# A hybrid attention layer on one core: the gate's activation ahead of the next x split in the first sweep, and a small transpose moved back in the output stage

## The chip, the core and the metric

The kernel runs on one core of one Trainium2 chip. The metric is the time of one execution in device microseconds (us), and the median of several runs is compared. The engines are called as in the profile: PE is TensorE, PEld its weight loads, ACT is ScalarE, DVE is VectorE, POOL is GpSimd, and SP is the engine that issues most of the DMAs.

## What is computed

One encoder layer over x with 2048 rows of 1024 numbers, all in float32. `x @ w_in` is cut by columns into the inputs of two groups of heads. Group A is gated linear attention in both directions over chunks of 64 positions, with a decay for each key dimension that comes from a product of low rank (`lr`), and a SiLU gate. Group B is latent attention with softmax over all positions, and a SiLU gate. Cut to what matters here:

```python
h = x @ w_in
g_q, g_k, g_v, g_gate, g_lr_f, g_lr_b, m_cq, m_ckv, m_kr, m_gate = split(h)
# group A, per direction
log_a = log_sigmoid(lr @ wg2 + bg) / 16
b = cumsum(log_a)                      # inside a chunk
q_dec, k_dec, k_tail = q * exp(b), k * exp(-b), k * exp(b_last - b)
o = mask(q_dec @ k_dec.T) @ v + q_dec @ state
state = state * exp(b_last) + k_tail.T @ v
o_a = rms_norm(o_fwd + o_bwd) * silu(gate)
# group B
o_b = softmax(q_nope @ k_nope.T + q_rope @ k_rope.T) @ v * silu(m_gate)
out = layer_norm(alpha * x + concat(o_a, o_b) @ w_out)
```

## The kernel before

**Number format.** [...]

**Stages.** The first sweep (`sweep_a`, to about 352 us) goes over the 16 tiles of 128 rows of x from the last to the first: step `i` works on tile `c = 15 - i`. It makes the inputs of group A and runs its forward half. A second sweep (to about 632 us) makes the inputs of group B and runs the backward half. Attention follows, 16 blocks of one head by 512 queries, block after block, and last the product with `w_out` and the LayerNorm, whose first parts run between the last block's work.

**A step of the first sweep.** For its tile it runs three product groups on PE, each over eight slices `k` of 128 of the 1024 input columns: `ipa_0` (288 columns: the decay's input `lr`, then `q`), `ipa_1` (384 columns: `k` and a part of `v`) and `ipa_2` (384 columns of `v`). Except for the tiles 15, 14 and 0, a fourth product `ipg` (512 columns: the gate) follows. Behind the three groups' products come copies out of PSUM: `ga_lr` copies `lr` in three pieces, `ga_q2` copies `q`. The four products take their PSUM banks in turn from one pool of two buffers, so the tile of `ipa_1` lies in the bank that `ipg` of the step before had. `gate_end` runs `silu` on `ipg`: three ACT passes (lines 1491, 1493, 1495) and a multiplication on DVE (line 1497) that reads `ipg` once more; the tile of the result is `gs`.

**Work between the products.** The smaller work of group A is called between the products at places that the table `STEPS_A` names: a key `(g, k)` means behind slice `k` of product group `g`, and each entry is a part and whether it belongs to the current step or to the one before it. `ga_q` transposes the copy of `q` on PE (`qT`), multiplies by the decay on DVE (`qd`, line 943), stores `qd` in four DMAs, and splits it into `qbh` and `qbl`, each in two halves. `ga_k` does the same for `kd` (line 967), `kh` and `kl`. `ga_kt` transposes `kd` (`kt`) and splits it. `ga_lrT` transposes `lr` and copies it out (`lrTs`), and `ga_z` multiplies it by the decay's weights (`z`). `ga_intra` is the masked product `Ap` of queries and keys, `ga_state` the product `Up` of keys and values. In the steps 5 to 9 of this loop parts of the rotary embedding's angles run too, and behind step 9 the sine and cosine tables, with two ACT table loads.

**The x tile.** At the head of step `i` the loop loads tile `i + 1` of x (`ga_ld`, into `xaf`) and splits it (`ga_x`): `xah` on ACT, `xal` on POOL. The last step does the same for the first tile of the second sweep (`xlate`).

**What sets the order.** The steps 0 to 3 follow a list written out by hand (`ORDER_A`). From step 4 on, each engine's order comes from the framework's scheduler at compile time, which starts from the order in the program and may move an instruction ahead of others; `self.after(i)` forbids it to put what is issued inside ahead of instruction `i`.

**The output stage.** In attention the order is written out by the table `PLACE`: for each part of a block a place in units of pairs of score products, behind the block's end for the late parts; a program sorts all parts by their places. Block 14 is the last but one. Its row sums are transposed in two small matmuls (`sx`, `tsum`, line 1658), reduced on DVE (line 1667) and inverted (`rc`, line 1669). `turn` (line 1680) transposes the four columns of reciprocals to four rows (`rt`); `rows` copies them on ACT (line 1686) and stores them on SP (line 1687). `y` is the block's product with the values' weights, and `yc` copies and stores it. `sx`, `y` and `rt` of that block take one PSUM bank in turn. `wof` (line 1848) is the load of the next slice of `w_out`, and `po` are the first parts of the output product.

## Time and profile before

| | |
|---|---|
| timed runs | 1296.20, 1297.36, 1297.93 us; median 1297.36 us |
| profiled execution | 1299.13 us, of which the span of the trace is 1296.9 us |
| busy, share of the span | PE 98%, PEld 86%, DVE 70%, ACT 65%, POOL 61% |
| granted clock of PE, mean over the span | 0.998 |
| instructions on PE | 6988 matmuls, 6988 weight loads |
| mean DMA rate over the span | 112 GB/s |

The windows of the profile give the stages. Each row is a stretch, its length, and the busy time of PE, PEld, DVE, ACT and POOL with their instructions, then the granted clock, the DMA share and GB/s:

```profile
22.00:132.00 110.00, 108.54 (x693) 103.22 (x693) 74.13 (x146) 71.86 (x159) 35.28 (x24) 1.00 0.30 92
132.00:352.00 220.00, 219.05 (x1358) 204.76 (x1358) 120.44 (x249) 131.72 (x284) 72.98 (x59) 1.00 0.27 81
1105.00:1297.00 192.00, 183.74 (x828) 152.68 (x828) 118.60 (x184) 54.10 (x141) 98.45 (x63) 0.98 0.55 176
```

The first two are the first sweep from its second step on, the last is the output stage. In a row of a timeline the first number is the start in us from the start of the span, the second the duration, and what stands in brackets is the idle time ahead of the instruction on its engine and what ended it. A matmul's duration reaches to its modelled end, so the next one starts before it is over; what a matmul costs PE is the distance between two starts.

### The profile page before, as it was taken

How to read it: one execution, taken by the hardware profiler on the slowest of the kernel's cores; microseconds unless marked ns; L12 is line 12 of the kernel's file. 1: busy time of each engine (PE TensorE's matmuls, PEld its weight loads, DVE VectorE, ACT ScalarE, POOL GpSimd, SP SyncE). 2: the span in 40 equal slices, each digit the busy share in tenths (PEclk: the TensorE clock that was granted, in tenths of full speed). 3: DMA queues.
4: the chain of work that ended last, by engine and by line, in shares of the span. 5: the costliest groups of instructions: out<-in, count | busy, mean ns of one | idle time of the engine just before them, and what ended most of it. 6: DMA issues, size and time to landing. Idle time of an engine off the chain costs nothing.

```text
span 1296.9 us, 19995 instructions
## 1 busy us (share of the span) xinstructions
PE 1270.2 (98%) x6988; PEld 1119.6 (86%) x6988; DVE 908.5 (70%) x1678; ACT 842.7 (65%) x1482; POOL 790.9 (61%) x500
## 2 busy tenths in 40 slices
PE   7999999999999999999999999999999999999997
PEld 7999999999889999999788888888888888788886
DVE  6865564445675455555898888888888888468655
ACT  7765657555675656655688888888888887523221
POOL 0243232232567666671288888889999999846550
PEclk9999999999999999999999999999999999999999
DMA  8232213131565555565401111122233110367752
GB/s 287 70 94 59 88 55 93 51 96 50 179 224 170 193 200 179 189 213 168 138 1 41 42 41 41 41 63 60 58 90 90 42 41 9 122 197 238 238 170 75
DMA packets 113444, 145.81 MB, mean 112 GB/s; under 512 B 17494, under 2 KB 70110, under 8 KB 113344
## 3 DMA queue, kind: packets, MB, share of 16 engines
q1 hardware_dynamic: 105184, 142.42, 34.9%
q0 software_dynamic: 768, 2.10, 0.4%
q8 instruction: 55, 0.90, 0.3%
q10 hardware_dynamic: 7392, 0.03, 0.3%
q14 instruction: 45, 0.37, 0.1%
HBM read 94.14 MB, written 50.36 MB: 111 GB/s over the span
## 4 chain that ended last, share of the span: by engine, by line
PE 86%; ACT 3%; DVE 2%; POOL 2%; issue 2%; DMA 1%; SPq 0%; DVEq 0%; ACTq 0%; POOLq 0%
PE o L424 4%; PE o L426 4%; PE pS L1535 4%; PE o L425 4%; PE pS L1537 4%; PE pS L1536 4%; PE pS L1538 4%; PE pS L1539 4%; PE ipa L424 4%; PE ipa L426 3%; PE ipa L425 3%; PE po L426 2%; PE po L425 2%; PE po L424 2%; PE pz L425 2%; PE pz L426 2%
## 5 line engine op out<-in xcount | busy, mean ns | idle before, releaser
L376 POOL TENSOR_TENSOR pl<-s,ph 128x1024 fp32r<-128x1024 f32 x128 | 306.3, 2417 | 58.0 <-ACT ph L370 58.0
L1557 DVE TENSOR_TENSOR rm<-pS,rm 128x512 f32<-128x512 f32 x210 | 144.8, 690 | 26.3 <-ACT s L1544 20.7
L1581 DVE TENSOR_TENSOR s<-s,mb 128x1024 f32<-128x1024 f32 x128 | 151.2, 1213 | 9.4 <-PE mb L1575 9.3
L1544 ACT ACTIVATE s<-pS 128x1024 f32<-128x1024 f32 x128 | 131.3, 1026 | 38.0 <-PE pS L1539 33.4
L1044 POOL TENSOR_TENSOR Us<-Us,cw 128x512 f32<-128x512 f32 x16 | 18.6, 1164 | 213.1 <-DVE Us L1042 181.3
L370 ACT ACTIVATE ph<-s 128x1024 fp32r<-128x1024 f32 x128 | 135.2, 1058 | 17.6 <-PE o L426 16.9
L1585 ACT ACTIVATE s<-s 128x1024 f32<-128x1024 f32 x128 | 131.5, 1051 | 13.4 <-DVE s L1581 13.3
L424 PE MATMUL ipa<-wah,xah 128*128 128x384 f32 (+1 forms) x384 | 131.1, 341 | 7.3 <-ACT wah L370 6.8
L425 PE MATMUL ipa<-wal,xah 128*128 128x384 f32 (+1 forms) x384 | 125.8, 327 | 0.2 <-DVE wal L376 0.2
L426 PE MATMUL ipa<-wah,xal 128*128 128x384 f32 (+1 forms) x384 | 125.0, 325 | 0.0
L1535 PE MATMUL pS<-qh,ckvT_h 128*128 128x512 f32 x256 | 102.5, 401 | 0.8 <-DVE rm L1557 0.4
L424 PE MATMUL o<-ph,vh 128*128 128x512 f32 x256 | 101.0, 395 | 0.0
L1536 PE MATMUL pS<-ql,ckvT_h 128*128 128x512 f32 x256 | 99.8, 390 | 0.0
L1538 PE MATMUL pS<-rh,krs 128*128 128x512 f32 x256 | 99.8, 390 | 0.0
L1537 PE MATMUL pS<-qh,ckvT_l 128*128 128x512 f32 x256 | 99.8, 390 | 0.0
L426 PE MATMUL o<-ph,vl 128*128 128x512 f32 x256 | 99.8, 390 | 0.0
L1539 PE MATMUL pS<-rl,krs 128*128 128x512 f32 x256 | 99.8, 390 | 0.0
L425 PE MATMUL o<-pl,vh 128*128 128x512 f32 x256 | 99.7, 390 | 0.0
L1608 DVE TENSOR_TENSOR ap<-ap,s 128x512 f32<-128x512 f32 x120 | 83.1, 692 | 7.1 <-ACT s L1585 4.5
L424 PEld LDWEIGHTS ipa<-wah,xah 128*128 128x128 f32 x384 | 73.1, 190 | 10.4 <-ACT wah L370 7.0
L376 POOL TENSOR_TENSOR ol<-of,oh 128x512 fp32r<-128x512 f32 x32 | 43.6, 1363 | 54.2 <-ACT oh L370 54.2
L424 PE MATMUL pz<-xch,wzh 128*128 128x256 f32 x256 | 74.8, 292 | 0.0
(327 smaller groups left out, 3830.1 us busy)
## 6 DMA issues: line engine op xcount, KB each, us to landing
xcf<-xT_dram SPq DMA_DIRECT2D x16, 512.0 KB, 5.3
xr<-x_dram SPq DMA_DIRECT2D x16, 512.0 KB, 5.7
out_dram<-rr SPq DMA_DIRECT2D x32, 256.0 KB, 4.9
xaf<-xT_dram SPq DMA_DIRECT2D x14, 512.0 KB, 3.8
oib<-oi_s SPq DMA_DIRECT2D x16, 256.0 KB, 3.8
qdb<-qd_s SPq DMA_DIRECT2D x16, 256.0 KB, 4.9
SU<-su_s SPq DMA_DIRECT2D x16, 256.0 KB, 4.1
ub<-u_s SPq DMA_DIRECT2D x16, 256.0 KB, 4.1
```

What stands on the lines that cost most here:

```text
L370: return nc.scalar.activation(dst, src, AF.Copy).ins
L376: return e.tensor_tensor(dst, src, hi.bitcast(F32), ALU.subtract).ins
L424: mm(out, ah, bh, start=start, stop=False)
L425: mm(out, ah, bl, start=False, stop=False)
L426: mm(out, al, bh, start=False, stop=stop)
L1535: mm(ps[:, e], kh, qh, start=True, stop=False)
L1536: mm(ps[:, e], kh, ql, start=False, stop=False)
L1537: mm(ps[:, e], kl, qh, start=False, stop=False)
L1538: mm(ps[:, e], kr, rh, start=False, stop=False)
L1539: mm(ps[:, e], kr, rl, start=False, stop=True)
L1557: V.tensor_tensor(d["rm"], src[:, e], d["rm"], ALU.max)
L1581: V.tensor_tensor(s, s, d["mb"][:, None, :].to_broadcast([P, 2, QB]), ALU.subtract)
```

## The change

It has three parts. First, in the loop steps of the first sweep only the load of the next x tile stays at the head of the step. Its split moves into a new part `next_x` behind slice 1 of `ipa_0`, and may not be put ahead of the last of the gate's three ACT passes. The multiplication `qd` may not be put ahead of the gate's multiplication on DVE. Second, `ga_q` and `ga_k` are cut in two. The transposes, the multiplications and the stores (`q1`, `k1`) stay behind slice 4 of `ipa_0`; the splits (`q3`, `k3`) go behind slice 1 of `ipa_1`, and `qbh` and `qbl` may not be put ahead of the copies of `lr`. Third, two places in `PLACE` put `turn` and `rows` of block 14 later.

```diff
-STEPS_A = {(0, 4): [("q", "prev"), ("k", "prev")], (1, 3): [("kt", "prev"), ("lrT", "cur")],
+STEPS_A = {(0, 1): [("next_x", "cur")], (0, 4): [("q1", "prev"), ("k1", "prev")], (1, 1): [("q3", "prev"), ("k3", "prev")], (1, 3): [("kt", "prev"), ("lrT", "cur")],
...
-    turn=13.6,
-    rows=13.65,
+    turn=17.5,
+    rows=17.55,
...
-                c = ch[i]["c"]
-                if c > 0:
-                    for f in (self.ga_ld, self.ga_x):
-                        for _ in f(i + 1):
-                            pass
+                if ch[i]["c"] > 0:
+                    for _ in self.ga_ld(i + 1):
+                        pass
                 else:
-                    self.xlate = [self.split_x(xp, self.load_x(NCH - 1, "xb"), NCH - 1, "xb")]
+                    self.xlate = self.load_x(NCH - 1, "xb")
...
-            self.hi(lr[:, 64:96], pt[:, 0:32])
+            h = self.hi(lr[:, 64:96], pt[:, 0:32])
             yield
-            self.lo(lr[:, 32:64], pt[:, 0:32], lr[:, 0:32])
+            self.lr_last = h, self.lo(lr[:, 32:64], pt[:, 0:32], lr[:, 0:32])
...
+    def ga_next_x(self, d):
+
+        with self.after(self.gate_act):
+            if d["c"] > 0:
+                for _ in self.ga_x(d["i"] + 1):
+                    pass
+            else:
+                self.xlate = [self.split_x(self.xab, self.xlate, NCH - 1, "xb")]
         yield
...
+        with self.after(*([self.gate_dve] if d["i"] > 3 else [])):
+            nc.vector.scalar_tensor_tensor(two(qd), qT[:, None, 0:2].to_broadcast([P, 2, 2, P]), 0.125, two(d["E1"]),
+                                           ALU.mult, ALU.mult)
...
+    def ga_q3(self, d):
+        qd, qbh, qbl = d["qd"], d["qbh"], d["qbl"]
         halves = (slice(0, 64), 0), (slice(64, 128), 1)
+        lr = self.lr_last if 3 < d["i"] < NCH - 1 else ()
         for r, j in halves:
-            self.hi(qbh[r, :, j], qd[r])
+            with self.after(*lr[:1]):
+                self.hi(qbh[r, :, j], qd[r])
             yield
         for r, j in halves:
-            self.lo(qbl[r, :, j], qd[r], qbh[r, :, j])
+            with self.after(*lr[1:]):
+                self.lo(qbl[r, :, j], qd[r], qbh[r, :, j])
             yield
...
-        self.nc.scalar.activation(t, t, AF.Exp, scale=-1.0)
+        self.gate_act = nc.scalar.activation(t, t, AF.Exp, scale=-1.0).ins
         yield 2
-        nc.vector.tensor_tensor(t, g, t, ALU.mult)
+        self.gate_dve = nc.vector.tensor_tensor(t, g, t, ALU.mult).ins
```

In the pieces below, what an instruction writes stands ahead of the arrow, the number at the end of a name counts the tile, and `x2` means that two like it follow each other. Line numbers behind the change are higher by up to 25. The first pair is ACT in an ordinary step of the first sweep, between the end of one gate product and the middle of `ipa_1`. Before:

```order
L370 ACTIVATE xah_2885<-xaf_2883 128x1024
L1491 ACTIVATE gs_2877<-ipg_2839 128x512
L1493 ACTIVATE gs_2877<-gs_2877 128x512
L1495 ACTIVATE gs_2877<-gs_2877 128x512
L370 ACTIVATE qbh_222<-qd_2908 64x4x128 x2
L370 ACTIVATE lr_221<-ipa_0_2889 128x32 x2
L370 ACTIVATE kh_2923<-kd_2921 128x512
L370 ACTIVATE q_4_2939<-ipa_0_2889 128x256
L370 ACTIVATE kth_2959<-kt_2954 128x2x4x64
```

and now, at the same place:

```order
L1516 ACTIVATE gs_2877<-ipg_2839 128x512
L1518 ACTIVATE gs_2877<-gs_2877 128x512
L1520 ACTIVATE gs_2877<-gs_2877 128x512
L370 ACTIVATE xah_2892<-xaf_2883 128x1024
L370 ACTIVATE lr_221<-ipa_0_2885 128x32 x2
L370 ACTIVATE qbh_222<-qd_2908 64x4x128
L370 ACTIVATE q_4_2931<-ipa_0_2885 128x256
L370 ACTIVATE qbh_222<-qd_2908 64x4x128
L370 ACTIVATE kh_2944<-kd_2917 128x512
L370 ACTIVATE kth_2959<-kt_2954 128x2x4x64
```

The split's copy `xah` has gone behind the gate's three passes, and the two copies of `lr` and the copy of `q` ahead of one half of `qbh` or both. DVE at the same place, before:

```order
L943 SCALAR_TENSOR_TENSOR qd_2908<-qT_2905,E_5_2745 128x512
L1497 TENSOR_TENSOR gs_2877<-ipg_2839,gs_2877 128x512
L967 TENSOR_TENSOR kd_2921<-kT_2918,E_5_2755 128x512
L376 TENSOR_TENSOR qbl_223<-qd_2908,qbh_222 64x4x128 x2
L376 TENSOR_TENSOR kl_2925<-kd_2921,kh_2923 128x512
L376 TENSOR_TENSOR lr_221<-ipa_0_2889,lr_221 128x32
```

and now:

```order
L1522 TENSOR_TENSOR gs_2877<-ipg_2839,gs_2877 128x512
L955 SCALAR_TENSOR_TENSOR qd_2908<-qT_2905,E_5_2745 128x512
L989 TENSOR_TENSOR kd_2917<-kT_2914,E_5_2755 128x512
L376 TENSOR_TENSOR lr_221<-ipa_0_2885,lr_221 128x32
L376 TENSOR_TENSOR qbl_223<-qd_2908,qbh_222 64x4x128 x2
L376 TENSOR_TENSOR kl_2946<-kd_2917,kh_2944 128x512
```

The gate's multiplication has changed places with `qd`, and the small subtraction of `lr` has gone from behind the three splits to ahead of them. The last pair is PE around `rt` of block 14, in the last block of attention. Before:

```order
L1658 MATMUL sx_12231<-ident,acc_12090 128x128 x2
L1680 MATMUL rt_12242<-ident,rc_12238 4x128
L424 MATMUL po_12135<-woh_10769,oh_0_11238 128x512
L425 MATMUL po_12135<-wol_10848,oh_0_11238 128x512
L426 MATMUL po_12135<-woh_10769,ol_0_11297 128x512
```

and now:

```order
L424 MATMUL o_12291<-ph_0_12214,vh 128x512
L425 MATMUL o_12291<-pl_0_12267,vh 128x512
L426 MATMUL o_12291<-ph_0_12214,vl 128x512
L1705 MATMUL rt_12298<-ident,rc_12238 4x128
L424 MATMUL o_12291<-ph_1_12242,vh 128x512
L425 MATMUL o_12291<-pl_1_12306,vh 128x512
```

`rt` has gone from right behind `sx` to behind `y` and a dozen further `po`, between two value products `o` of the last block. On SP the store of `rt` stood ahead of the load `wof`, and the store of `yc` came behind both; now the order is `wof`, `yc`, `rt`.

More of the change, by code (lines that the diff above doesn't have):

```diff
@@ L810, in ga_x @@
         self.lo(xl[:, :, 0], xf, xh[:, :, 0], "dve" if i < 4 else "pool")
+        yield
+    def ga_next_x(self, d):
[5 more added lines that the diff above has]
+                self.xlate = [self.split_x(self.xab, self.xlate, NCH - 1, "xb")]
         yield
@@ L933, in ga_q, with ga_q1 @@
     def ga_q(self, d):
+        yield from self.ga_q1(d)
+        yield from self.ga_q3(d)
+    def ga_q1(self, d):
         nc, c = self.nc, d["c"]
-        qbh, qbl = d["qbh"], d["qbl"]
         qT = d["tr"].tile([P, H, P], F32, tag="tr", name=f"qT{c}")
@@ L940, in ga_q @@
         yield
-        qd = self.t512(d, "qd")
+        qd = d["qd"] = self.t512(d, "qd")
         two = lambda t: t.rearrange("p (r q) t -> p r q t", r=2)
-        nc.vector.scalar_tensor_tensor(two(qd), qT[:, None, 0:2].to_broadcast([P, 2, 2, P]), 0.125, two(d["E1"]),
-                                       ALU.mult, ALU.mult)
+        with self.after(*([self.gate_dve] if d["i"] > 3 else [])):
+            nc.vector.scalar_tensor_tensor(two(qd), qT[:, None, 0:2].to_broadcast([P, 2, 2, P]), 0.125, two(d["E1"]),
+                                           ALU.mult, ALU.mult)
         dst = self.qd_s[c].rearrange("(r d) (q g t) -> r g d q t", r=2, q=2, g=2)
@@ L949, in ga_q, with ga_k1 @@
         yield
+    def ga_q3(self, d):
+        qd, qbh, qbl = d["qd"], d["qbh"], d["qbl"]
         halves = (slice(0, 64), 0), (slice(64, 128), 1)
+        lr = self.lr_last if 3 < d["i"] < NCH - 1 else ()
         for r, j in halves:
-            self.hi(qbh[r, :, j], qd[r])
+            with self.after(*lr[:1]):
+                self.hi(qbh[r, :, j], qd[r])
             yield
         for r, j in halves:
-            self.lo(qbl[r, :, j], qd[r], qbh[r, :, j])
+            with self.after(*lr[1:]):
+                self.lo(qbl[r, :, j], qd[r], qbh[r, :, j])
             yield
     def ga_k(self, d):
+        yield from self.ga_k1(d)
+        yield from self.ga_k3(d)
+    def ga_k1(self, d):
         nc, c = self.nc, d["c"]
@@ L968, in ga_k, with ga_k3 @@
         yield
+    def ga_k3(self, d):
+        kd = d["kd"]
         kh = d["kh"] = self.t512(d, "kh", dt=F32R)
@@ L1494, in silu @@
         yield 1
-        nc.scalar.activation(t, t, AF.Exp, scale=-1.0)
+        self.gate_act = nc.scalar.activation(t, t, AF.Exp, scale=-1.0).ins
         yield 2
-        nc.vector.tensor_tensor(t, g, t, ALU.mult)
+        self.gate_dve = nc.vector.tensor_tensor(t, g, t, ALU.mult).ins
         yield 3
```

## The prediction

> **What bounds the kernel now.** I read the page's busy times first, then the waits of TensorE, then the timelines of one sweep step and of the stretch around the moved transpose, last the windows with the granted clock.

> ```profile
> PE 1270.2 (98%) x6988; PEld 1119.6 (86%) x6988; DVE 908.5 (70%) x1678; ACT 842.7 (65%) x1482; POOL 790.9 (61%) x500
> ```

> TensorE (PE) is busy 98% of the span: 26.7 us are all that it stands. So an edit gains what it takes from PE's standing time, and loses what it adds there. The waits (who waited for whom: total us, times, longest) of PE's weight loads and of its matmuls name two that the change touches.

> ```profile
> PEld ipa L424 <- DVE gs L1497: 2.8, 12, 0.7
> PE rt L1680 <- DVE rc L1669: 3.3, 1, 3.3
> ```

> The first comes once in each of 12 sweep steps: `ipa_1` takes the PSUM bank that the gate product `ipg` of the step before filled, and DVE's `gs` multiplication is that bank's last reader. One such step (start, duration):

> ```profile
> 239.37 0.39 PE L426 MATMUL ipg<-wgh,xal 128*128 128x512 f32 x1
> 239.57 1.06 ACT L370 ACTIVATE xah<-xaf 128x1024 fp32r<-128x1024 f32 x1 [1.97 <-PE ipg L425]
> 240.53 0.58 ACT L1491 ACTIVATE gs<-ipg 128x512 f32<-128x512 f32 x1
> 240.76 2.40 POOL L376 TENSOR_TENSOR xal<-xaf,xah 128x1024 fp32r<-128x1024 f32 x1 [2.05 <-ACT xah L370]
> 241.81 0.63 ACT L1495 ACTIVATE gs<-gs 128x512 f32<-128x512 f32 x1
> 242.60 0.68 DVE L1497 TENSOR_TENSOR gs<-ipg,gs 128x512 f32<-128x512 f32 x1
> 243.09 0.30 PE L426 MATMUL ipa<-wah,xal 128*128 128x288 f32 x1
> 243.34 0.44 PE L424 MATMUL ipa<-wah,xah 128*128 128x384 f32 x1
> 243.62 0.34 PE L425 MATMUL ipa<-wal,xah 128*128 128x384 f32 x1
> 243.79 0.34 PE L426 MATMUL ipa<-wah,xal 128*128 128x384 f32 x1
> ```

> The split's first pass `xah` stands ahead of the gate's three passes, and DVE's `gs` ends at 243.28. PE should go on 0.14 after 243.09, at 243.23, but starts at 243.34, and its next spacing is 0.28 instead of 0.17: 0.22 us lost per step.

> **The change, part 1: gate ahead of the split.** The last `ipg` matmul ends at 239.76, so the first gate pass can start at 239.80. The three take 1.91 (240.53 to 242.44), `gs` on DVE, now ahead of `qd`, runs 241.75 to 242.43, and PE wants the bank at 243.23. The wait goes, with 0.8 to spare: 0.22 gained in each ordinary step. The split is the cover that has to be found again: it runs at 241.77 on ACT and 242.96 to 245.36 on POOL, and the next step needs it some 16 us later. The load after next now leaves SP behind four `qd` stores and when that buffer is free, 245.4 instead of 243.2, with 18 us in hand: nothing.

> **Part 2: gate input ahead of query and key splits.** These rows say what comes next.

> ```profile
> 242.72 1.29 ACT L370 ACTIVATE qbh<-qd 64x512 fp32r<-64x512 f32 x2 [0.28 <-DVE qd L943]
> 243.80 1.39 DVE L376 TENSOR_TENSOR qbl<-qd,qbh 64x512 fp32r<-64x512 f32 x2
> 244.03 0.29 ACT L370 ACTIVATE lr<-ipa 128x32 fp32r<-128x32 f32 x2
> 244.34 0.63 ACT L370 ACTIVATE kh<-kd 128x512 fp32r<-128x512 f32 x1
> 245.22 0.69 DVE L376 TENSOR_TENSOR kl<-kd,kh 128x512 fp32r<-128x512 f32 x1
> 245.54 0.60 PE L981 MATMUL kt<-ident,kd 128*128 128x128 f32 x4
> 246.33 0.59 ACT L370 ACTIVATE kth<-kt 128x512 fp32r<-128x512 f32 x1
> 246.80 0.28 ACT L370 ACTIVATE lrTs<-lrT 98x128 fp32r<-98x128 f32 x1
> 247.16 0.64 PE L883 MATMUL z<-lrTs,wg 98*128 98x128 f32 x4
> 248.97 0.28 PE L426 MATMUL Ap<-qbh,kl 128*128 128x256 f32 x1
> ```

> ACT is free of the split at 242.73 (`xah` advances 0.96), but `ipa_0` ends at 243.39, so `lr` starts at 243.42 and 0.7 of the split is hidden there. Then, by the spacings of these rows: `qbh` 243.73, `q` 244.38, `qbh` 244.67, `kh` 245.33. `kt` on PE, 0.22 earlier, ends at 245.92, `kth` starts at 245.95, `lrTs` ends at 246.70. `z` is due at 246.94: 0.24 in hand.

> DVE is the tighter question, because POOL's split now lies beside `qbl` and `kl` instead of beside `qd` and `gs`. A step where POOL works beside `qbl` (the last row is the group: min/median/max ns):

> ```profile
> 89.11 1.04 POOL L1069 TENSOR_TENSOR Sb<-Sb,cw 64x512 f32<-64x512 f32 x1
> 89.22 2.20 DVE L376 TENSOR_TENSOR qbl<-qd,qbh 64x512 fp32r<-64x512 f32 x2
> L376 DVE TENSOR_TENSOR qbl<-qd,qbh x32: 669/687/1682, 33.3 to 347.4; 64x512 fp32r<-64x512 f32 x32
> ```

> One `qbl` took 1.68 instead of 0.69: 0.93 until POOL's `Sb` ended at 90.15, and then its own time. `gs` at 242.60, with one input in PSUM, lost nothing beside `xal`. So I let `qbl` wait for the end of `xal`: 245.36, then two halves 1.42, `kl` 246.78 to 247.47. `Ap` wants `kl` at 248.75: 1.3 in hand in an ordinary step. [...]

> Two of the 12 steps differ.

> ```profile
> 87.97 0.19 PEld L424 LDWEIGHTS ipa<-wah,xah 128*128 128x128 f32 x1 [0.72 <-DVE gs L1497]
> 222.04 1.28 ACT L608 ACT_TABLE_LOAD   x1
> 225.56 0.29 PE L425 MATMUL Ap<-qbl,kh 128*128 128x256 f32 x1
> 228.19 0.34 PE L424 MATMUL ipa<-wah,xah 128*128 128x384 f32 x1
> ```

> The first one gets back 0.72 + 0.11 = 0.83, but there one half of `qbl` stands ahead of `lr` on DVE and, blocked until `Sb` ends, holds `lrT` back by about 0.6: +0.2, between +0.8 (no block) and −2.2 (`xal` gets in first too, 2.4 more). In the step with two ACT table loads the split now follows them: the second load ends at 223.32 less the gate's advance of 0.73 (240.53 to 239.80 above), 222.6, `xal` runs 223.8 to 226.2, `qbl` ends at 227.6, and the `Ap` matmul that ran at 225.56 waits for it. Behind it come, by their spacings in PE's timeline between the last two rows, `z` (0.47) and ten `Ap` at 0.117, to about 229.75, and by then four `ipa_2` at 0.17 (0.70) are done; before, PE stood at that place at 228.19 with one `Up` done (0.11). Loss 1.0, between −1.4 and +0.2 (no block). Sweep: 10 × 0.22 + 0.2 − 1.0 = 1.4 us gained.

> **Part 3: the transpose `rt` of block 14.**

> ```profile
> 1101.62 0.40 PE L1658 MATMUL sx<-ident,acc 128*128 128x128 f32 x2
> 1104.51 0.41 DVE L1667 TENSOR_REDUCE rc<-sx 128x4 f32<-128x256 f32 x1
> 1105.28 0.27 PE L1680 MATMUL rt<-ident,rc 128*4 128x128 f32 x1 [3.26 <-DVE rc L1669]
> 1109.61 0.51 PE L424 MATMUL y<-ofh,wv_h 128*128 128x512 f32 x1
> 1106.00:1110.00 4.00, 4.00 (x13) 3.10 (x12) 3.97 (x6) 2.04 (x3) 2.38 (x1) 0.57 0.38 132
> 1110.00:1115.00 5.00, 5.00 (x24) 4.13 (x23) 3.94 (x6) 2.44 (x4) 4.11 (x2) 1.00 0.32 72
> ```

> In the windows the figure behind the five engines' busy times is the granted clock: after the 3.26 us wait it is 0.57 for four microseconds, then 1.00, so 4.00 × 0.43 = 1.7 us are lost to the clock while the twelve `po` matmuls run, from 1105.3 to 1109.6. With `rt` gone from there, PE goes from `sx` straight to these twelve and would reach `y` at 1109.61 − 3.26 − 1.7 = 1104.6. `y` takes the PSUM bank that `sx` used, free when the reduce ends at 1104.92: `y` starts at 1105.0 instead of 1109.61, 4.6 earlier. `rt` itself then costs 0.15 between two value products. It also waits for the copy of `y`, since it takes that bank next: on ACT behind two `ph` and one `woh` at about 1108.2, PE comes at 1109.5. Gain 4.45, of which 1.7 is clock.

> Nothing in hand must then be late: SP, where the `wof` load stood behind `rt`'s store.

> ```profile
> 1105.88 0.27 SPq L1687 DMA_DIRECT2D r_s<-rt  x1
> 1106.24 0.35 SPq L1848 DMA_DIRECT2D wof<-wO_dram  x1
> 1178.78 0.48 PE L424 MATMUL pmb<-woh,oh 128*128 128x512 f32 x1
> 1180.42 1.30 POOL L376 TENSOR_TENSOR ol<-of,oh 128x512 fp32r<-128x512 f32 x1 [0.74 <-ACT oh L370]
> ```

> The load leaves some 4 us earlier as well. The tightest later place is the split ending at 1181.72, wanted by `pmb`'s fifteenth matmul at 1182.05; its loads start when PE frees buffers, so I let it move along.

> **Sum.** 1.4 + 4.45 = 5.85. The profiled execution took 1299.13 (span 1296.9, 2.2 around it) and would take 1293.3; the median of the timed runs is 1297.36, which gives 1291.5. The ends: sweep −1.4 (−2.2 − 1.4 + 2.2) to 3.2 (2.2 + 0.8 + 0.2), attention 2.75 (no clock part) to 4.9 (no wait at `y`).

> **The rivals.**
> - The half clock is not in every run. The pause at `rt` may meet the clock differently in the timed runs; the trace has one instance. Gain 1.4 + 2.75: 1293.2. [...]
> [...]
> - The tail is paced by loads, not PE: the split at 1180.42 stays where it is, 0.33 in hand, and PE gives the 4.45 back. 1296.0, no change. Against it: the buffers that start these loads are freed by PE.
> - Slower: `z` waits for `lrTs`. If ACT is not idle before `lr`, the split's 0.96 comes onto its path; less 0.24 in hand, plus 0.10 refill, 0.82 in each of 12 steps, 9.8 us: 1301.3. It outweighs the gains from 0.5 us per step on, and passes 0.2% from 0.7. For it: `xah` now stands right ahead of `lr`; against it, ACT is free 0.7 before `ipa_0` ends.
> - The change does not free the bank (another reader is last): no 0.22 per step, 1293.7.

> **How the numbers follow.** Forecast 1291.5, chance 0.50, its own range 1290.3 to 1293.0; clock 0.12; port 0.14; paced tail 0.12; `z` 0.08; bank 0.04. A measurement tells about 0.2% (2.6 us) from no change, so faster means under 1294.8: 0.50 + 0.12 + 0.14 + 0.04 = 0.80; same 0.12; slower 0.08. The range takes in all but `z` and the far end of some: 1289.2 to 1296.2.

> **What would show it.** Right: no row `ipa L424 <- DVE gs` among PE's waits; `rt` without a wait, `y` waiting some 0.3 for the reduce, granted clock 1.00 there; `qbl` at about 1.6 us beside `xal`; a wait of over 1 us of `Ap` in the table step. Wrong: `z` waiting for `lrTs` in each step, `Ap` waiting for `kl` in ordinary steps, `pmb` or `po` waiting for `ol` or `wol` behind 1105, or `rt` waiting for the copy of `y`.

## The result, and the profile after

The changed kernel takes 1292.22 us in the median (1291.05 to 1293.28, 6 runs), the kernel before beside it 1297.28: a ratio of 0.9962, 95% interval 0.9949 to 0.9974, so 3.4 to 6.6 us less. In the fifth experiment, where both kernels ran anew, it was 0.9950 (0.9937 to 0.9962). The forecast of 1291.5 lies 0.7 from the first median. The profiled execution took 1291.78 with a span of 1290.0, 6.9 less than the span before; but the profiled execution of before, 1299.13, was itself 1.9 above its median, so that the traces' difference is larger than that of the medians.

PE's busy time and its waits, from the page and the waits of PE's matmuls:

```profile
PE 1265.4 (98%) x6988; PEld 1118.1 (87%) x6988; DVE 921.0 (71%) x1678; ACT 840.9 (65%) x1482; POOL 791.2 (61%) x500
...
PE Ap L425 <- DVE qbl L376: 1.1, 1, 1.1
PE Ap L426 <- DVE kl L376: 1.1, 2, 0.7
...
PE y L424 <- DVE rc L1692: 0.3, 1, 0.3
```

The rows `ipa <- DVE gs` and `rt <- DVE rc` are gone. New are one wait of `Ap` for `qbl`, a second one for `kl`, and the short one of `y` for the reduction. DVE is busy 12.5 us more although it does the same work: that is time in which it stands inside an instruction, and 12.2 of it lie in `qbl`.

The timeline of the ordinary step that the prediction showed (everything is about 0.9 earlier by then). Line 370 is `hi`, the copy that rounds a float32 tile, and line 376 `lo`, the subtraction that holds what the rounding lost; lines 424 to 426 are the three matmuls of a product of two tiles split in this way (`mm3`).

```profile
240.80 1.04 ACT L370 ACTIVATE xah<-xaf 128x1024 fp32r<-128x1024 f32 x1
240.92 0.69 DVE L1522 TENSOR_TENSOR gs<-ipg,gs 128x512 f32<-128x512 f32 x1 [3.43 <-ACT gs L1520]
241.97 2.40 POOL L376 TENSOR_TENSOR xal<-xaf,xah 128x1024 fp32r<-128x1024 f32 x1 [3.85 <-ACT xah L370]
242.13 0.68 DVE L989 TENSOR_TENSOR kd<-kT,E 128x512 f32<-128x512 f32 x1
242.93 0.19 DVE L376 TENSOR_TENSOR lr<-ipa,lr 128x32 fp32r<-128x32 f32 x1
243.43 2.20 DVE L376 TENSOR_TENSOR qbl<-qd,qbh 64x512 fp32r<-64x512 f32 x2 [0.32 <-ACT qbh L370]
245.64 0.27 ACT L370 ACTIVATE lrTs<-lrT 98x128 fp32r<-98x128 f32 x1
245.67 0.69 DVE L376 TENSOR_TENSOR kl<-kd,kh 128x512 fp32r<-128x512 f32 x1
246.13 0.56 PE L891 MATMUL z<-lrTs,wg 98*128 98x128 f32 x4
```

`gs` ends at 241.61, well ahead of `ipa_1`. `xal` runs to 244.37, and the two halves of `qbl` take 2.20 instead of 1.39. A view of DVE alone that ends ahead of the second half shows the first:

```profile
243.43 1.48 DVE L376 TENSOR_TENSOR qbl<-qd,qbh 64x512 fp32r<-64x512 f32 x1 [0.32 <-ACT qbh L370]
```

It takes 1.48 instead of 0.69: 0.94 until `xal` ends and 0.54 behind it. `kd`, which reads PSUM, took its usual 0.68 beside the same `xal`. So the first half of `qbl`, whose two inputs lie in SBUF, waited for `xal` and ended 0.54 behind it, and `kd` lost nothing.

What four ordinary steps cost, from the start of `z` in one to the start of `z` four steps on, first before, then after:

```profile
113.81 0.63 PE L883 MATMUL z<-lrTs,wg 98*128 98x128 f32 x4
202.12 0.63 PE L883 MATMUL z<-lrTs,wg 98*128 98x128 f32 x4
```

```profile
113.38 0.56 PE L891 MATMUL z<-lrTs,wg 98*128 98x128 f32 x4
200.42 0.56 PE L891 MATMUL z<-lrTs,wg 98*128 98x128 f32 x4
```

88.31 against 87.04: 0.32 a step, where the forecast had 0.22. The step with the table loads:

```profile
222.04 2.39 POOL L376 TENSOR_TENSOR xal<-xaf,xah 128x1024 fp32r<-128x1024 f32 x1 [7.29 <-ACT xah L370]
222.62 3.07 DVE L376 TENSOR_TENSOR qbl<-qd,qbh 64x512 fp32r<-64x512 f32 x2 [0.32 <-ACT qbh L370]
225.75 0.39 PE L425 MATMUL Ap<-qbl,kh 128*128 128x256 f32 x1 [1.15 <-DVE qbl L376]
```

`qbl` waits inside its 3.07 for `xal` to end at 224.43, and `Ap` waits 1.15 for `qbl`. The first loop step:

```profile
89.16 2.72 POOL L376 TENSOR_TENSOR xal<-xaf,xah 128x1024 fp32r<-128x1024 f32 x1
89.76 2.67 DVE L376 TENSOR_TENSOR qbl<-qd,qbh 64x512 fp32r<-64x512 f32 x1
92.46 0.69 DVE L376 TENSOR_TENSOR kl<-kd,kh 128x512 fp32r<-128x512 f32 x1
93.20 0.38 PE L426 MATMUL Ap<-qbh,kl 128*128 128x256 f32 x1 [0.33 <-DVE kl L376]
```

Here `xal` gets in between the halves of `qbl`, the second takes 2.67, and `Ap` waits for `kl`. `xal` itself, which starts beside the first half, takes 2.72 instead of 2.40. Last, block 14 and the windows behind it (the figure behind the five busy times is the granted clock):

```profile
1098.62 0.41 PE L1683 MATMUL sx<-ident,acc 128*128 128x128 f32 x2
1102.08 0.47 PE L424 MATMUL y<-ofh,wv_h 128*128 128x512 f32 x1 [0.29 <-DVE rc L1692]
1106.92 0.27 PE L1705 MATMUL rt<-ident,rc 128*4 128x128 f32 x1
1102.00:1106.00 4.00, 3.92 (x17) 3.30 (x18) 3.97 (x6) 3.15 (x4) 3.15 (x2) 1.00 0.00 1
1106.00:1110.00 4.00, 4.00 (x19) 3.20 (x18) 3.79 (x6) 2.77 (x4) 4.00 (x3) 1.00 0.36 100
```

From `sx` to `y` it takes 3.46 instead of 7.99, with the clock at 1.00, and `rt` waits for nothing.

### The profile page after: what moved, and what is told of

Same layout as the page of the kernel before. It is cut to its first block, busy times and chain, and to the rows that moved or that the text cites. A ratio compares the mean times of both kernels' runs of the same rounds, so it can differ in the third digit from the quotient of the medians.

```text
span 1290.0 us, 19998 instructions
## 1 busy us (share of the span) xinstructions
PE 1265.4 (98%) x6988; PEld 1118.1 (87%) x6988; DVE 921.0 (71%) x1678; ACT 840.9 (65%) x1482; POOL 791.2 (61%) x500
## 4 chain that ended last, share of the span: by engine, by line
PE 87%; ACT 3%; DVE 2%; POOL 2%; issue 1%; DMA 1%; SPq 0%; DVEq 0%; ACTq 0%; POOLq 0%
PE o L426 4%; PE o L424 4%; PE pS L1560 4%; PE o L425 4%; PE pS L1561 4%; PE pS L1562 4%; PE pS L1563 4%; PE pS L1564 4%; PE ipa L424 3%; PE ipa L426 3%; PE ipa L425 3%; PE pz L425 2%; PE po L426 2%; PE po L425 2%; PE po L424 2%; PE pz L424 2%
## 5 line engine op out<-in xcount | busy, mean ns | idle before, releaser
L376 POOL TENSOR_TENSOR pl<-s,ph 128x1024 fp32r<-128x1024 f32 x128 | 306.1, 2415 | 56.7 <-ACT ph L370 56.7
L370 ACT ACTIVATE ph<-s 128x1024 fp32r<-128x1024 f32 x128 | 134.9, 1057 | 13.5 <-PE o L426 12.9
L424 PE MATMUL ipa<-wah,xah 128*128 128x384 f32 (+1 forms) x384 | 129.9, 338 | 6.7 <-ACT wah L370 6.7
L1069 POOL TENSOR_TENSOR Us<-Us,cw 128x512 f32<-128x512 f32 x16 | 18.6, 1163 | 181.7 <-DVE Us L1067 166.2
L425 PE MATMUL ipa<-wal,xah 128*128 128x384 f32 (+1 forms) x384 | 124.7, 325 | 0.2 <-DVE wal L376 0.2
L426 PE MATMUL ipa<-wah,xal 128*128 128x384 f32 (+1 forms) x384 | 124.7, 325 | 0.0
L424 PE MATMUL o<-ph,vh 128*128 128x512 f32 x256 | 101.1, 395 | 0.0
L426 PE MATMUL o<-ph,vl 128*128 128x512 f32 x256 | 99.8, 390 | 0.0
L425 PE MATMUL o<-pl,vh 128*128 128x512 f32 x256 | 99.7, 389 | 0.0
L424 PEld LDWEIGHTS ipa<-wah,xah 128*128 128x128 f32 x384 | 72.9, 190 | 7.6 <-ACT wah L370 7.0
L376 POOL TENSOR_TENSOR ol<-of,oh 128x512 fp32r<-128x512 f32 x32 | 43.4, 1356 | 53.2 <-ACT oh L370 53.2
L424 PE MATMUL pz<-xch,wzh 128*128 128x256 f32 x256 | 74.8, 292 | 0.0
```

The lines of the kernel that those rows point to most:

```text
L370: return nc.scalar.activation(dst, src, AF.Copy).ins
L376: return e.tensor_tensor(dst, src, hi.bitcast(F32), ALU.subtract).ins
L424: mm(out, ah, bh, start=start, stop=False)
L425: mm(out, ah, bl, start=False, stop=False)
L426: mm(out, al, bh, start=False, stop=stop)
```

## The experiments

### Each part alone

The changed kernel with the old places of `rt`, and the kernel before with the new ones:

```diff
# first: the changed kernel
-    turn=17.5,
-    rows=17.55,
+    turn=13.6,
+    rows=13.65,
# second: the kernel before
-    turn=13.6,
-    rows=13.65,
+    turn=17.5,
+    rows=17.55,
```

Expected of the first:

> The first sweep's two parts as in the change, the transpose rt and its store back at their old places. By the prediction's terms 1.4 us less than before (1295.9), by what the changed kernel's trace shows in the sweep 2.0 us less (1295.3); rt waits about 3.3 us again, and if the half clock belongs to that pause, the granted clock is below 0.7 for the four microseconds behind it. Rival, the clock's phase decides: the pause is there and the clock stays at 1.00 in this trace.

Expected of the second:

> Only rt and its store moved, the sweep as before. If the half clock behind the pause is in most runs, 4.45 us less than before: 1292.8. Rival, the half clock is in few runs: 2.75 less, 1294.5. Rival, the tail is paced by loads: no change, 1297.3. The wait of ipa_1 for gs is there in all 12 steps.

The sweep alone: 1295.97 against 1297.79, ratio 0.9987 (0.9978 to 0.9995), 1.7 us less. `rt` alone: 1293.43, ratio 0.9966 (0.9953 to 0.9978), 4.4 us less, the forecast's 4.45; the interval, 2.9 to 6.1, just leaves out the 2.75 of the rival without the half clock. In its trace the wait for `gs` is there 12 times (2.8 us together), as expected, and `y` waits 0.3 for the reduction. In the trace of the first, `rt` stands as before, and the windows from 1097 on:

```profile
1098.32 0.41 PE L1683 MATMUL sx<-ident,acc 128*128 128x128 f32 x2
1101.99 0.37 PE L1705 MATMUL rt<-ident,rc 128*4 128x128 f32 x1 [3.26 <-DVE rc L1694]
1107.28 0.63 PE L424 MATMUL y<-ofh,wv_h 128*128 128x512 f32 x1
1097.00:1102.00 5.00, 1.74 (x10) 1.11 (x9) 3.21 (x8) 3.20 (x4) 3.93 (x2) 0.90 0.00 0
1102.00:1107.00 5.00, 5.00 (x13) 3.93 (x14) 4.97 (x6) 2.53 (x4) 2.38 (x1) 0.50 0.36 105
1107.00:1112.00 5.00, 5.00 (x22) 4.05 (x21) 3.65 (x6) 2.23 (x3) 4.18 (x2) 0.92 0.17 60
```

The same pause of 3.26 brings the half clock again, so the rival in which the clock stays at 1.00 does not hold here. It comes sooner and for longer: 0.10, 0.50 and 0.08 of 5 us each are lost, so it holds for about 6.8 us against 3.4 before, and `y` comes 8.96 behind `sx` instead of 7.99. So the price of this wait is not one number, and a trace of before with one instance could not have told that.

### The gate first, but without the second part

The second part is taken out of the changed kernel: `q` and `k` stay whole, and `lr` has no place ahead of them.

```diff
-(0, 4): [("q1", "prev"), ("k1", "prev")], (1, 1): [("q3", "prev"), ("k3", "prev")],
+(0, 4): [("q", "prev"), ("k", "prev")],
...
-        lr = self.lr_last if 3 < d["i"] < NCH - 1 else ()
+        lr = ()
```

> As the changed kernel, but query and key splits stay whole at their old place, ahead of lr's subtraction on DVE. If POOL's xal holds DVE's qbl back until it ends, lr's subtraction comes 1.6 us later than lrT on PE wants it in each ordinary step: about 11 x 1.6 = 18 us slower than the changed kernel, near 1310, with lrT waiting for lr 11 times. Rival, xal holds back nothing: the subtraction comes at the time that PE wants it and the kernel is as fast as the changed one, 1292.2.

It took 1318.76 us, ratio 1.0156 (1.0139 to 1.0173) to the kernel before. Its waits of PE, and an ordinary step:

```profile
PE lrT L879 <- DVE lr L376: 18.1, 11, 3.4
```

```profile
256.51 2.40 POOL L376 TENSOR_TENSOR xal<-xaf,xah 128x1024 fp32r<-128x1024 f32 x1 [4.09 <-ACT xah L370]
257.45 2.73 DVE L376 TENSOR_TENSOR qbl<-qd,qbh 64x512 fp32r<-64x512 f32 x2
260.82 0.18 DVE L376 TENSOR_TENSOR lr<-ipa,lr 128x32 fp32r<-128x32 f32 x1
261.05 0.32 PE L879 MATMUL lrT<-ident,lr 128*98 128x128 f32 x1 [1.42 <-DVE lr L376]
```

The chain stands there as expected: `xal` to 258.91, `qbl` behind it, `kl`, and only then the small subtraction of `lr` that PE waits for, in 11 steps. The gate ahead of the split is worth nothing without the second part: the kernel is 21 us slower than before although `rt` is moved in it too, so with the 4.4 of `rt` added the gate's move alone costs some 25 us, an estimate. The expectation of 1310 left out the first loop step, in which the wait is 3.38 and brought the half clock here too (0.50 between 96 and 98 us). The traced execution, 1315.14, was the fastest of four. The other three took 3.5 to 4.8 more, at a mean granted clock of 0.991 to 0.992 against 0.998 in the traced one; that the half clock came behind more of their 11 waits is likely, but not shown.

### POOL's split behind `kl`

```diff
-(1, 1): [("q3", "prev"), ("k3", "prev")]
+(1, 1): [("q3", "prev"), ("k3", "prev"), ("next_xl", "cur")]
...
+    def ga_next_xl(self, d):
+        if d["c"] > 0:
+            next(d["xg"])
+            self.tc.add_manual_dep(self.xl_ins, self.kl_ins.name, mybir.DependencyInfo(
+                mybir.DependencyClass.Sync, mybir.DependencyReason.DATA), reason="xal behind kl")
```

Here `next(d["xg"])` issues the `lo` of the next x tile, which is `xal`.

> As the changed kernel, but POOL's xal also waits for DVE's kl, so that it lies beside none of qbl and kl. If the block by xal is what the first loop step and the table-load step pay, qbl takes 0.69 each everywhere, Ap no longer waits 1.15 us for qbl in the table-load step nor 0.33 for kl in the first, and lrT less in the first: 1.5 to 2.0 us less than the changed kernel, 1290.2 to 1290.7. Rival, those waits have another cause (the table loads, Sm and Sb on POOL alone): no change, 1292.2.

It took 1289.50 us, ratio 0.9935 (0.9924 to 0.9946) to the kernel before, 8.4 us less; the time lies 0.7 below the range that was expected. The table step in its trace:

```profile
222.24 0.68 DVE L376 TENSOR_TENSOR qbl<-qd,qbh 64x512 fp32r<-64x512 f32 x1 [0.32 <-ACT qbh L370]
223.17 0.69 DVE L376 TENSOR_TENSOR qbl<-qd,qbh 64x512 fp32r<-64x512 f32 x1 [0.24 <-ACT qbh L370]
224.81 2.40 POOL L376 TENSOR_TENSOR xal<-xaf,xah 128x1024 fp32r<-128x1024 f32 x1 [10.41 <-DVE kl L376]
```

Each half of `qbl` has its own 0.69 again. `Ap` waits for `qbl` nowhere, and for `kl` in the first loop step no longer; the two short waits of `lrT` for `lr` stay, 0.7 together, which was not expected. In the first loop step the cause is not `xal`: the half of `qbl` ahead of `lr` lies beside POOL's `Sb` and still takes 1.20. Set against the changed kernel's trace, PE gains 0.6 over the first loop step and 1.4 over the table step, 2.0 as expected.

### The changed kernel again, and one step further

The changed kernel was run once more beside the next two, and the version above with the reduction of block 14 put into the time in which DVE waits for `ofh`, the rounded part of the operand of `y`:

```diff
-put(NP * i + NP - 1 + at(n, i), f, i)
+put(NP * i + NP - 1 + (12.9 if (n, i) == ("rcp", nb - 2) else at(n, i)), f, i)
```

> The changed kernel itself, on the chip and beside the runs of the next two: 5 us less than the kernel before if the first comparison holds, 6.1 if the two parts measured alone (1.7 and 4.4) add up.

> The version with xal behind kl, and in block 14 the reduction rc on DVE ahead of ofl, in the idle time in which DVE waits for ofh. Theory: xal behind kl is worth 1.5 to 2.7 us beside the changed kernel on the same chip, and y's wait of 0.3 us for rc is gone: 1.8 to 3.0 less than the changed kernel. Rival, the gain of xal behind kl was the chip's: no more than 0.5 less.

The changed kernel: 1291.59 against 1297.77, 6.2 less (by the ratio's interval 4.9 to 8.2), as the two parts add up. The further version: 1288.51, ratio 0.9927 (0.9915 to 0.9939), 3.1 us less than the changed kernel beside it and the fastest of all. In its trace `y` no longer waits:

```profile
1095.93 0.41 PE L1690 MATMUL sx<-ident,acc 128*128 128x128 f32 x2
1097.24 0.42 DVE L1699 TENSOR_REDUCE rc<-sx 128x4 f32<-128x256 f32 x1
1098.93 0.39 PE L424 MATMUL y<-ofh,wv_h 128*128 128x512 f32 x1
```

3.00 from `sx` to `y` against 3.46. That the two together bring 3.1 and not 2.0 + 0.5 is within the spread of the five runs on each side (1290.35 to 1292.77 against 1288.04 to 1289.19). A likely part of it is in the second trace of the changed kernel, in the windows behind the table step's wait:

```profile
225.00:226.00 1.00, 1.00 (x8) 1.00 (x8) 1.00 (x2) 0.00 (x0) 0.00 (x0) 0.95 0.95 283
226.00:227.00 1.00, 1.00 (x6) 1.00 (x6) 0.40 (x2) 0.81 (x2) 0.00 (x0) 0.50 0.52 209
...
228.00:229.00 1.00, 1.00 (x5) 1.00 (x5) 0.00 (x0) 0.60 (x2) 0.00 (x0) 0.50 0.00 0
229.00:230.00 1.00, 1.00 (x7) 1.00 (x6) 0.97 (x2) 0.70 (x2) 0.00 (x0) 0.84 0.00 0
```

Behind the same wait of 1.15 us, which cost no clock in the first trace, the clock was halved for 3.4 us, from 225.9 to 229.3: 1.7 us more for this step in that execution.

### A shorter pause at `rt`

In the kernel before, six of the twelve `po` are put ahead of `rt`, so that the pause shrinks and little work moves.

```diff
-    turn=13.6,
-    rows=13.65,
+    turn=14.455,
+    rows=14.456,
...
-put(end + (out["part"][k] if k else place), op.part, o, k)
+put(end + (out["part"][k] + 0.01 * o["c"] * (k == 2) if k else place), op.part, o, k)
```

> The kernel before with rt behind six of the twelve po instead of behind none, so that PE's pause is about 1.9 us instead of 3.3; only 1.36 us of work goes ahead of it. If a pause of 1.9 us does not bring the half clock, the granted clock stays at 1.00 and y comes 3.0 us earlier after sx than before, the kernel is about 3 us faster (1294.4). Rival, any pause of this sort brings it: y comes 1.4 us earlier and the kernel is 1.4 us faster (1296.0).

```profile
1100.18 0.41 PE L1658 MATMUL sx<-ident,acc 128*128 128x128 f32 x2
1103.85 0.27 PE L1680 MATMUL rt<-ident,rc 128*4 128x128 f32 x1 [1.87 <-DVE rc L1669]
1105.64 0.63 PE L424 MATMUL y<-ofh,wv_h 128*128 128x512 f32 x1
1105.00:1106.00 1.00, 1.00 (x4) 0.78 (x3) 1.00 (x2) 1.00 (x2) 1.00 (x1) 0.50 0.01 2
1108.00:1109.00 1.00, 1.00 (x5) 0.77 (x5) 1.00 (x2) 0.71 (x1) 1.00 (x1) 0.80 0.38 143
```

The pause is 1.87, and the half clock comes all the same, from 1105.0 to 1108.4; most of it lies behind the start of `y` now. `y` comes 5.46 behind `sx` instead of 7.99: 2.5 earlier, and neither 1.4 nor 3.0. In this execution the rival holds in that the half clock comes, and its time, 1296.32, is near the rival's 1296.0. The median is 1295.64 against 1297.77, ratio 0.9982 (0.9973 to 0.9991): 2.3 us less, between the 1.4 and the 3.0, as if a part of the executions kept the full clock. How large that part is, is open.

## Why the prediction was right

- **The wait for `gs`** went in every step, as forecast. Its 0.22 is right: in the ordinary step shown the last `ipa_0` and the first two `ipa_1` start within 0.31, where it was 0.53 before. But a step gained 0.32. Most of the rest is PE's: the four `z` take 0.56 instead of 0.63, where `lrTs` ends 0.22 ahead of them and no longer 0.08, and `lrT` stands directly behind `kt`, so that `ipa_1` is interrupted once less. The prediction took the second part as a thing that may cost and not as one that may gain.
- **The block by POOL's `xal`** was the step that mattered most, and it held: each of the 11 halves of `qbl` that start beside `xal` ends 0.54 to 0.56 behind it, and where the fourth experiment puts `xal` behind `kl`, that is gone. That it blocks less, the 0.14 that the chances give to `port`, fell: no run shows a port, and what the traces show is this wait. But the row that it was read from was misread, see below.
- **The table step** lost 1.0 in the trace, as forecast: from the `z` at 200.42 to the next but one at 246.13 it is 45.71 against 45.04, 0.67 more, although one of these two steps is ordinary and gains 0.32. `Ap` waits 1.15, forecast over 1; the start of `xal` was put at 223.8 and came at 222.04, of which PE's lead of 1.1 there is the larger part. What the prediction lacked is the half clock behind this wait, another 1.7 in one of the two traces.
- **The first loop step** was forecast at +0.2, between +0.8 and −2.2. By the starts on PE, the changed kernel is 0.36 ahead when it begins, 0.82 at its `z`, and 0.22 at the gate product behind it: 0.1 lost. `lrT` waited 0.32 and not 0.6. But `xal` got in between the halves of `qbl`, half-way to the case that the lower end of the range stands for, and `Ap` paid 0.33 for `kl`, which the sum had not charged.
- **Sweep together**: 1.4 forecast, 2.0 by the starts of `z` in the trace, 1.7 (0.6 to 2.9) measured alone. That the sum came so near is in part luck: ten ordinary steps gained 1.0 more than forecast, the first loop step 0.3 less, and the half clock behind the table step took 1.7 in one of the two traces.
- **`rt`**: `y` comes 4.53 earlier behind `sx`, forecast 4.6; its wait for the reduction is 0.29, forecast some 0.3; `rt` waits for nothing. 4.45 forecast, 4.4 measured alone. That 1.7 of it is clock was one draw: 1.7 in the trace before, and in the trace of the sweep alone 2.9, half of the 5.8 us of half clock behind the start of `rt`.
- **The tail** kept the gain, but for a few tenths: PE leads by 7.4 us at the first `pmb` of the output product and the span ends 6.9 sooner. The rival that loads pace it fell.
- **`z` waiting for `lrTs`** did not come: `lrTs` ends at 245.91, and `z` starts at 246.13, 0.22 in hand where 0.24 was forecast.

The prediction gave 1.68 us to the `qbl` that lies beside `Sb`. That is the longest of the 32 `qbl`, the one at 347.4; the one beside `Sb` took 1.48, and with the second half the 2.20 of its row:

```profile
89.22 1.48 DVE L376 TENSOR_TENSOR qbl<-qd,qbh 64x512 fp32r<-64x512 f32 x1
```

It is 0.93 until `Sb` ended and 0.55 behind it, 0.14 short of a full block with a whole 0.69 behind it, where 1.68 would be 0.06 over it. The ordinary steps behind the change show the same: 1.48 to 1.54, with 0.54 to 0.56 behind the end of `xal`. So the waiting was read rightly from the wrong row; why the part behind it is shorter than 0.69 stays open.

## What to carry to other kernels

When a piece of work on GpSimd is moved out of one wait's way, look which VectorE instructions it will lie beside: here each half of `qbl`, with two inputs in SBUF, that started beside `xal` took until 0.54 to 0.56 us behind its end (2.67 us instead of 0.69 at the worst), and a single slow instance in the trace was enough to see it coming. The pause of 3.26 us cost more than its length, since the clock dropped behind it, and how much differed from trace to trace (1.7 us in that of before, 3.4 us in that of the sweep alone); so a term that holds a half clock needs a range, and filling the pause with ready work was worth more here than shortening it (4.4 us against 2.3). Before a reordering is called done, ask what the moved cover collides with at its new place: here a wait on `kl` for POOL's split, and the reduction in DVE's idle time, brought 3.1 us beyond the change.

## What the runs showed of the hardware

What PE did ahead of a drop can be counted in the traces. Lay a grid of 3.413 us through the start of a half clock, and add up the columns (the last number of a matmul's shape) that PE's matmuls stream in each stretch of it, each matmul's spread over its duration; the sums are estimates, since the ends of matmuls are modelled.

| trace | stretch, us | columns | clock behind it |
|---|---|---|---|
| gate without the second part | 91.77 to 95.18 | 1750 | half |
| sweep alone | 1097.55 to 1100.96 | 2090 | half |
| sweep alone, the next stretch | 1100.96 to 1104.38 | 2660 | still half |
| before | 1103.03 to 1106.44 | 2260 | half |
| shorter pause at `rt` | 1101.58 to 1104.99 | 2940 | half |
| changed, second trace | 222.49 to 225.90 | 3220 | half |
| gate without the second part | 187.34 to 190.76 | 3260 | full |
| changed, first trace | 224.64 to 228.06 | 4170 | full |

The six with half behind them are all such stretches in the nine traces between 10 and 1279 us, and 3260 is the emptiest with full behind it; the median is 7420. So in these traces the drops lie behind 3220 columns and fewer, though 3220 and 3260 lie closer together than these sums can be trusted. The same wait of 1.15 us cost 1.7 us in the trace of the changed kernel where its stretch held 3220 columns, and nothing in the one where it held 4170; and the 6.8 us came where the pause of 3.26 left two stretches in a row with 2090 and 2660. In the third experiment several stretches with a wait of 1.4 us lie just above that (3260, 3300, 3330, 3390 and 3400), so a small shift of the grid could bring the half clock there in its slower executions; no trace shows those.
